# Input norm and MLP norm of a decoder layer: transposes one tile ahead, a split gain row, and row factors moved behind the MLP

## The chip, the cores and the metric

The kernel runs on one core of a Trainium2 chip. A run's time is the device time of one execution in microseconds. The profile is one execution taken by the hardware profiler; its span runs from the first to the last instruction.

## The reference, cut to what matters

One decoder layer on 512 tokens of width 1024, in float32. An RMS norm feeds one wide projection, whose parts go to an mLSTM branch and to a sliding-window attention branch. The two are gated, merged and projected back onto `x`. Then a squared-ReLU MLP, a gated per-layer input and a last RMS norm follow.

```
def rmsnorm(x, g):
    return x * rsqrt(mean(x * x, axis=-1) + EPS) * g

h = rmsnorm(x, norm_mix_g);  proj = h @ w_in          # 1024 -> 6664, split into nine parts
...                                                    # mLSTM branch y_a, window attention y_b
merged = sigmoid(g_a) * (y_a @ w_branch_a) + sigmoid(g_b) * (y_b @ w_branch_b)
x = x + merged @ w_out
u = rmsnorm(x, norm_mlp_g) @ w_up                      # 1024 -> 4096
x = x + square(relu(u)) @ w_down                       # 4096 -> 1024
gate = sigmoid(rmsnorm(x, norm_ple_g) @ w_ple_gate)
x = x + gate * (p @ w_ple_proj)
return rmsnorm(x, final_norm_g)
```

## The kernel before, in words

Each big product is made of three products of fp32r parts. `split` casts a value to its high part on ScalarE (L134) and subtracts to get the low part on VectorE (L135); `pairs` then gives high x high, high x low and low x high. Weights arrive on SyncE's DMA queue as raw tiles `wr`, four at a time, and become `wh` and `wl`. The program is written as plain calls; a scheduler that works with estimated durations sets the order of each engine's queue when the kernel is built. `tc.issue_after(ins)` adds an edge of order, without a wait: what the block issues on that instruction's engine comes behind it. `tc.keep_in_program_order` pins an instruction's place.

**The input norm (L249 to L292).** The four tiles of 128 tokens come in as `xt`. The gain row `grow` is spread over all partitions by two plain float32 products with a row of ones (L251), into the PSUM tile `gmix`. For each tile, ScalarE squares and sums (L268), takes the root (L256), VectorE takes the reciprocal (L258) and makes `xn = x * rs * gmix` in two halves (L272). TensorE transposes `xn` in eight blocks into two PSUM banks (L279). Each bank is split into the high and low part of `h`, and ScalarE copies it once more into `hf`, the full-precision `h` (L284). Then come the 24 products of the tile with the weight `w_vsif`, which was split in three pieces by `load_w` within tile 0, and the results `vs` and `gt` are taken out. `hf` is read later by the sums `s1` to `s4`, which the value and gate projections use.

**The MLP (L841 to L977).** `x1` holds the transposed, gain-scaled `x` in parts, without the row factor of the norm. The row factors `rstd` of the four tiles are spread to all partitions by four plain products with a scaled identity `dg` (L859) into `rB`. The MLP goes in four quarters, each an up stage and a down stage. In `up`, 24 products fill a PSUM bank, VectorE makes `max(ps, 0) * rB` (L879), ScalarE squares it into `F` (L883), and sums of blocks of `F` are split into `uf`. `down` uses seven products per block instead of eight, with the PSUM pairs X, Y and Z. Each finished pair is added to `x` in one 1024-wide add (`acc`, L916); the product `p1` that several blocks share is summed over the quarters and added three times in the last one (`acc_p1`).

Of the kernel before, what the change touches and what calls it, by code (L numbers as in the profile page):

```python
# [16 lines left out]
P = 128  # L17
# [19 lines left out]
def block_kernel(  # L37
# [59 lines left out]
    def ps_a():  # L97
        return pp.tile([P, 1024], F32, tag="a", bufs=2, name=nm("psa"))
# [29 lines left out]
    def r32(t):  # L128
        return t.bitcast(F32)
# [66 lines left out]
    V.memset(ones, 1.0)  # L196
    eps_t = cp.tile([P, 1], F32, name="eps_t")

    cp.tile([P, 24], F32, name="pad")
    V.memset(eps_t, EPS)  # L200
    zeros4 = c1.tile([4, P], F32, name="zeros4")
    V.memset(zeros4, 0.0)
# [43 lines left out]
    nc.sync.dma_start(out=bif, in_=b_if.broadcast_to([P, 8]))  # L246
    sink = c1.tile([P, 16], F32, name="sink")
    nc.sync.dma_start(out=sink, in_=sinks.broadcast_to([P, 16]))
    gmix = ps_a()  # L249
    for c in range(2):  # L250
        T.matmul(gmix[:, c * 512 : (c + 1) * 512], ones[:1, :], grow[:, c * 512 : (c + 1) * 512], start=True, stop=True)  # L251
    def rstd_of(ss, n):

        w = ss.shape[1]
# [6 lines left out]
    vs = []  # L261
    gt = c1.tile([P, NT, 8], F32, name="gt")
    h2, hT = big_hl("h")
    hf = []
    for m in range(NT):
        xn = tok_scratch("xn")
        ss = small("ss", 1)
        A.activation(xn, xt[m], AF.Square, accum_out=ss)  # L268
        rs = rstd_of(ss, D)
        for c in range(2):  # L270
            o = slice(c * 512, (c + 1) * 512)
            V.scalar_tensor_tensor(xn[:, o], xt[m][:, o], rs, gmix[:, o], ALU.mult, ALU.mult)  # L272
        hf.append(tk("hf")[:, :D].rearrange("p (k c) -> p k c", k=KT))
        if m == 0:
            wv = [load_w(None, (k.stop - k.start) * 264, k.stop - k.start, w) for k, w in zip(K3, wv)]
        for kq in range(2):
            ps = ps_t()
            for k in range(4):
                T.transpose(ps[:, k * P : (k + 1) * P], xn[:, kq * 512 + k * P : kq * 512 + (k + 1) * P], ident)  # L279
            split(  # L280
                [t[:, 4 * kq : 4 * kq + 4, m * P : (m + 1) * P] for t in h2],
                ps.rearrange("p (k c) -> p k c", k=4),
            )
            A.copy(hf[m][:, 4 * kq : 4 * kq + 4, :], ps.rearrange("p (k c) -> p k c", k=4))  # L284

        ps = ps_g()
        for c in range(3):
            mm_tok(ps[:, :264], wv[c], hT[K3[c]], m, first=c == 0, last=c == 2)
        t = sp.tile([P, 256], F32, tag="vs", bufs=4, name=nm("vs"))
        A.copy(t, ps[:, :256])  # L290
        V.tensor_add(gt[:, m, :], ps[:, 256:264], bif)
        vs.append(t)  # L292

    def proj_T(wd, i, bank=ps_g):
# [77 lines left out]
    o_proj(1)  # L372


    vm = []
    for m in range(NT):
        t = tk("vm").rearrange("p (h d) -> p h d", h=NH)
        G.memset(t[:, :, DV : DV + 1], 1.0)
        vm.append(t)

    def h_part(tok, par):

# [52 lines left out]
    def seven(form, prod, X, Y, Z, b, post):  # L435


        b11, b12, b21, b22 = b
        n = range(len(b11))
        for i in n:  # L440
            prod(X, A11, form(b11[i]), i, True)
        post("p1", X)
        for i in n:
            V.tensor_sub(b12[i], b22[i], b12[i])
            V.tensor_add(b11[i], b12[i], b11[i])
        for i in n:
# [18 lines left out]
        post("c21", Y)  # L465

    def vml():
        raws = quads(w_vml, ["wr", "wr", "lm", "lm", "wr", "wr", "lm", "lm"])
# [380 lines left out]
    rB = mp.tile([P, 512], F32, name="rB")  # L849
    p1 = np_.tile([P, 2, 512], F32, name="p1")  # L850

    psr = pair()[:, 0, :]
    for m in range(NT):
        junk = np_.tile([P, 7 * 256], F32, tag="uf", bufs=8, name=nm("junk"))[:, :D]
        ss = small("ss", 1)
        A.activation(junk, xk[m], AF.Square, accum_out=ss)
        dg = mp.tile([P, 512], F32, tag="rt", bufs=3, name=nm("dg"))[:, :P]
        V.tensor_scalar_mul(dg, ident, rstd_of(ss, D))
        T.matmul(psr[:, m * P : (m + 1) * P], ones, dg, start=True, stop=True)  # L859
    A.copy(rB, psr)  # L860

    def load_down(q):
        raws = []
# [9 lines left out]
    def up(q, uf):  # L873
        fs = None
        for f in range(8):
            ps = ps_g()
            mm_T(ps, load_w(w_up[q * 8 + f], KT * P, KT), x1)
            a = mp.tile([P, 512], F32, tag="rt", bufs=3, name=nm("rt"))
            V.scalar_tensor_tensor(a, ps, 0.0, rB, ALU.max, ALU.mult)  # L879
            if f % 2 == 0:  # L880
                fs = F()
            o = 2 * (f % 2)
# [14 lines left out]
    def down(q, uf):  # L897
# [13 lines left out]
                    ops += pairs([h[:, o : o + P] for h in uf[2 * kh + k]], [h[:, k, :] for h in w])  # L911
                chain(ps[:, t, :], ops, first and kh == 0, last and kh == 1, True)

        def acc(ps, toks, n):
            o = XK[:, 2 * toks : 2 * toks + 2, n * 512 : (n + 1) * 512]
            return V.tensor_add(o, ps, o)  # L916

        def acc_p1(toks, n):
            if q == 3:
                tc.keep_in_program_order(acc(p1, toks, n))  # L920

        for kh in range(2):
            V.tensor_sub(b12[kh], b22[kh], b12[kh])
# [261 lines left out]
```

## Time and profile before

| what | value |
|---|---|
| median of three runs | 908.59 us (907.73, 908.59, and one of 1108.4) |
| the profiled execution, its own time | 907.79 us |
| its span | 906.0 us |
| TensorE busy | 890.4 us, 98% of the span |
| weight loads on TensorE | 739.4 us |
| VectorE busy | 640.6 us, 71% |
| ScalarE busy | 452.8 us, 50% |
| GpSimd busy | 25.0 us, 3% |
| DMA | 101.51 MB, mean 112 GB/s |

The busy time of an engine is the time in which one of its instructions runs. Engines work side by side, so these times overlap. A row of a group gives the line, the engine, the operation, what it writes and reads with shapes, the count, then the busy time and the mean of one in nanoseconds, and then the idle time ahead of it with what ended that. A row of the chain gives a start, a length, and the engine and line that set the end there. A row of the timeline gives a start, a length and the instruction, and in brackets the idle time ahead of it. Names are as in this page: PE is TensorE, PEld its weight loads, DVE VectorE, ACT ScalarE, POOL GpSimd, SP SyncE.

### The profile page before, as it was taken

What the parts mean: (1) busy time and instruction counts of PE and PEld (TensorE: products, weight loads), DVE (VectorE), ACT (ScalarE), POOL (GpSimd) and SP (SyncE); (2) the same over time, 40 slices, a digit from 0 to 9 for tenths busy, and PEclk for the clock granted to TensorE, in tenths of its full rate; (3) what the DMA queues carried; (4) which work ended last, traced back from release to release, by engine and by line L of the source; (5) the groups of instructions that cost most, each with busy time, mean ns of one, the idle gap of its engine ahead of it and who ended that gap; (6) DMA issues with size and microseconds to landing.
All of it is one profiled execution on the core that took longest, in us unless ns stands there. A gap on an engine that the chain in (4) does not pass through costs nothing.

```text
span 906.0 us, 11754 instructions
## 1 busy us (share of the span) xinstructions
PE 890.4 (98%) x4490; PEld 739.4 (82%) x4490; DVE 640.6 (71%) x1020; ACT 452.8 (50%) x757; POOL 25.0 (3%) x44
## 2 busy tenths in 40 slices
PE   7999999999999999999999999999999999999996
PEld 5888889998877677777888888888888888888886
DVE  6684687874787977466654678857966895799556
ACT  6573444454677567564322545334434533454753
POOL 0011000000000000000210000000000000000000
PEclk9999999999999999999999999999999999999998
DMA  6644124435211122234452520531162044201402
GB/s 235 241 156 151 59 81 167 162 117 173 71 49 69 47 96 92 76 110 140 163 186 93 207 95 1 198 127 47 54 225 94 0 159 146 69 24 64 145 1 93
DMA packets 30346, 101.51 MB, mean 112 GB/s; under 512 B 4301, under 2 KB 4813, under 8 KB 30290
## 3 DMA queue, kind: packets, MB, share of 16 engines
q1 hardware_dynamic: 28002, 93.15, 29.9%
q0 software_dynamic: 2144, 7.35, 2.3%
q8 instruction: 35, 0.57, 0.2%
q10 hardware_dynamic: 144, 0.26, 0.1%
q14 instruction: 21, 0.17, 0.1%
HBM read 91.30 MB, written 8.40 MB: 110 GB/s over the span
## 4 chain that ended last, share of the span: by engine, by line
PE 93%; ACT 2%; DVE 2%; DMA 1%; issue 0%; SPq 0%; ACTq 0%; DVEq 0%
PE psg L162 51%; PE psp L162 23%; PE psa L162 10%; PE pst L724 2%; PE pst L653 1%; PE pst L162 1%; PE psa L645 1%; PE pst L714 1%; PE psa L608 1%; PE psa L609 1%; DMA xt<-in_x 1%; DMA gfin<-in_g_fin 1%; PE psp L817 1%; ACT jk L736 1%; ACT pT L647 0%
## 5 line engine op out<-in xcount | busy, mean ns | idle before, releaser
L134 ACT CAST wh<-wr 128x1024 fp32r<-128x1024 f32 (+1 forms) x137 | 142.9, 1046 | 207.7 <-PE psg L162 75.4
L135 DVE TENSOR_TENSOR wl<-wr,wh 128x1024 fp32r<-128x1024 f32 (+1 forms) x137 | 173.4, 1270 | 102.4 <-ACT wh L134 95.4
L162 PE MATMUL psg<-x,wh 128*128 128x512 f32 x512 | 158.4, 390 | 0.0
L162 PE MATMUL psp<-wh,uf 128*128 128x512 f32 x448 | 139.2, 390 | 0.0
L162 PEld LDWEIGHTS psg<-x,wh 128*128 128x128 f32 x512 | 96.1, 188 | 19.8
L162 PE MATMUL psg<-h,wh 128*128 128x512 f32 x320 | 101.3, 395 | 0.0
L162 PE MATMUL psg<-x,wl 128*128 128x512 f32 x256 | 99.7, 390 | 0.0
L162 PEld LDWEIGHTS psp<-wh,uf 128*128 128x128 f32 x448 | 84.1, 188 | 17.4
L162 PE MATMUL psp<-wl,uf 128*128 128x512 f32 x224 | 87.3, 390 | 0.0
L134 ACT CAST wh<-wd 128x1024 fp32r<-128x1024 f32 x44 | 46.3, 1054 | 58.0 <-PE psp L162 26.1
L162 PEld LDWEIGHTS psg<-h,wh 128*128 128x128 f32 x320 | 58.8, 188 | 15.9 <-issue 4.9
L162 PE MATMUL psg<-h,wl 128*128 128x512 f32 x160 | 62.9, 393 | 0.0
L135 DVE TENSOR_TENSOR wl<-wd,wh 128x1024 fp32r<-128x1024 f32 x44 | 53.5, 1219 | 4.4 <-ACT wh L134 4.1
L162 PEld LDWEIGHTS psg<-x,wl 128*128 128x128 f32 x256 | 48.1, 188 | 9.8
L162 PE MATMUL psa<-h,wh 128*128 128x256 f32 (+1 forms) x256 | 55.2, 312 | 0.0
L162 PEld LDWEIGHTS psp<-wl,uf 128*128 128x128 f32 x224 | 42.1, 188 | 8.6
L135 DVE TENSOR_TENSOR uf<-F,uf 128x1792 fp32r<-128x1792 f32 (+2 forms) x20 | 33.0, 1650 | 21.8 <-ACT uf L134 21.8
L162 PEld LDWEIGHTS psa<-h,wh 128*128 128x128 f32 x256 | 41.9, 191 | 3.5 <-ACT p L533 0.7
L162 PE MATMUL psg<-yb,wh 128*128 128x512 f32 x128 | 42.8, 409 | 0.0
L134 ACT CAST uf<-F 128x1792 fp32r<-128x1792 f32 (+2 forms) x20 | 27.9, 1395 | 26.4 <-DVE F L893 26.2
L162 PE MATMUL psg<-ya,wh 128*128 128x512 f32 x128 | 40.6, 394 | 0.0
L879 DVE SCALAR_TENSOR_TENSOR rt<-psg,rB 128x512 f32<-128x512 f32 x32 | 22.0, 688 | 25.6 <-PE psg L162 25.6
(273 smaller groups left out, 1673.3 us busy)
## 6 DMA issues: line engine op xcount, KB each, us to landing
wr<-in_w_up SPq DMA_DIRECT2D x32, 512.0 KB, 3.2
wd<-in_w_down SPq DMA_DIRECT2D x24, 512.0 KB, 3.8
wr<-in_w_o SPq DMA_DIRECT2D x8, 512.0 KB, 4.5
gd<-gr POOLq DMA_DIRECT2D x8, 512.0 KB, 2.9
wr<-in_w_qsw SPq DMA_DIRECT2D x8, 512.0 KB, 4.3
wr<-in_w_qkml SPq DMA_DIRECT2D x8, 512.0 KB, 3.3
wr<-in_w_b SPq DMA_DIRECT2D x8, 512.0 KB, 3.2
gl<-gd SPq DMA_DIRECT2D x8, 512.0 KB, 3.4
```

The costliest lines, as they stand in the source:

```text
L134: A.copy(dst[0], src)
L135: V.tensor_sub(dst[1], src, r32(dst[0]))
L162: last_mm[0] = T.matmul(ps, l, r, start=first and i == 0, stop=last and i == len(ops) - 1, skip_group_check=parts)
L608: T.matmul(o, q[:, n * P : (n + 1) * P], kk[kp][ab][:, k0 : k0 + 256], start=True, stop=False)
L609: T.matmul(o, q[:, n * P : (n + 1) * P], kl[kp][ab][:, k0 : k0 + 256], start=False, stop=True)
L645: T.transpose(pt[:, c : c + P], lm3[ab][:, g, j * P : (j + 1) * P], ident)
L653: T.matmul(o[HALF[ab], :], vs[n + 1 - nk + j][:, c : c + 64], pTs[j][:, ab * 512 : (ab + 1) * 512], start=j == 0, stop=j == nk - 1,)
L714: T.matmul(psc[:, n0:], qk[4 + h][:, n0 : n0 + P], qk[h][:, n0:], start=True, stop=True)
L724: T.matmul(pn[:, : DV + 1], wT[s][:, t * P : (t + 1) * P], vm[s][:, h, :], start=s == 0, stop=s == t)
L736: A.activation(jk[:, :DV], h_of(h, t), AF.Square, scale=rd[:, t : t + 1], accum_out=hss[:, h, t : t + 1])
L817: T.transpose(ps[:, m * P : (m + 1) * P], xk[m][:, k * P : (k + 1) * P], ident)
L879: V.scalar_tensor_tensor(a, ps, 0.0, rB, ALU.max, ALU.mult)
```

## The change

In the input norm:

- `grow` is split into two fp32r parts, and `gmix` is the sum of four fp32r products with an fp32r row of ones, in place of two plain ones. Nine plain 128x128 products of ones with ones (`stir`) stand before, between and behind them.
- The loop over tiles is taken apart into `norm` and `columns`. The norm and the transposes of tile m+1 are written ahead of the products of tile m. Odd tiles transpose into one two-bank tile and are cast, subtracted and copied 1024 wide.
- The high part of `w_vsif` is made by GpSimd. The low part of its first piece is ordered behind tile 0's norm on VectorE, the other two behind tile 1's norm. Tile 1's norm is ordered behind tile 0's casts on ScalarE, tile 2's behind tile 1's subtraction on VectorE.
- `hf` of tiles 1 to 3 is copied by ScalarE as before; `hf` of tile 0 is the sum of both parts of `h`, made by VectorE after the last `gt`. `vm` takes its buffers later.

In the MLP: the factors `r2 = 1 / (mean(x*x) + EPS)` stay one column per tile. The rectifier runs on ScalarE without a factor, and since relu(u r)^2 = r^2 relu(u)^2, the factor is applied to the rows of the down products, as each accumulation into `x` becomes two 512-wide `ps * r2 + x`. `rB`, `dg` and the four products go.

```diff
+    idle = ps_g()
+
+    def stir(n):
+        for i in range(n):
+            tc.keep_in_program_order(T.matmul(idle[:, :P], ones, ones, start=True, stop=True))
+
+    one_row = c1.tile([1, P], F32R, name="one_row")
+    A.copy(one_row, ones[:1, :])
     gmix = ps_a()
+    gparts = [[act_r("gm")[:1, :] for _ in range(2)] for _ in range(2)]
     for c in range(2):
-        T.matmul(gmix[:, c * 512 : (c + 1) * 512], ones[:1, :], grow[:, c * 512 : (c + 1) * 512], start=True, stop=True)
+        split(gparts[c], grow[:, c * 512 : (c + 1) * 512])
+    stir(5)
+    for i in range(2):
+        for c in range(2):
+            tc.keep_in_program_order(
+                T.matmul(gmix[:, c * 512 : (c + 1) * 512], one_row, gparts[c][i], start=i == 0, stop=i == 1, skip_group_check=True)
+            )
+        stir(1 if i == 0 else 3)
...
+    def norm(m):
         xn = tok_scratch("xn")
         ss = small("ss", 1)
         A.activation(xn, xt[m], AF.Square, accum_out=ss)
         rs = rstd_of(ss, D)
         for c in range(2):
             o = slice(c * 512, (c + 1) * 512)
-            V.scalar_tensor_tensor(xn[:, o], xt[m][:, o], rs, gmix[:, o], ALU.mult, ALU.mult)
+            done = V.scalar_tensor_tensor(xn[:, o], xt[m][:, o], rs, gmix[:, o], ALU.mult, ALU.mult)
+        return xn, done.ins
...
+    def columns(m, xn):
+
+        if m % 2:
+            ps = ps_a()
+            halves = [ps[:, :512], ps[:, 512:]]
+        else:
+            halves = [ps_t(), ps_t()]
+        for k in range(KT):
+            T.transpose(halves[k // 4][:, k % 4 * P : (k % 4 + 1) * P], xn[:, k * P : (k + 1) * P], ident)
+        n = 8 if m % 2 else 4
+        for k in range(0, KT, n):
+            dst = [t[:, k : k + n, m * P : (m + 1) * P] for t in h2]
+            src = (ps if m % 2 else halves[k // 4]).rearrange("p (k c) -> p k c", k=n)
+            first = A.copy(dst[0], src)
+            second = V.tensor_sub(dst[1], src, r32(dst[0]))
+            if m:
+                if k == 0:
+                    hf.append(tk("hf")[:, :D].rearrange("p (k c) -> p k c", k=KT))
+                A.copy(hf[m][:, k : k + n, :], src)
+        return first.ins, second.ins
+
+    def load_vs_w(c):
+        n = K3[c].stop - K3[c].start
+        hl = [wp.tile([P, 1024], F32R, tag=t, bufs=WB, name=nm(t))[:, : n * 264] for t in ("wh", "wl")]
+        G.tensor_copy(hl[0], wv[c][:, : n * 264])
+        V.tensor_sub(hl[1], wv[c][:, : n * 264], r32(hl[0]))
+        return [q.rearrange("p (k c) -> p k c", k=n) for q in hl]
+
+    xn, normed = norm(0)
+    with tc.issue_after(normed):
+        wv[0] = load_vs_w(0)
+    on_scalar, _ = columns(0, xn)
+    with tc.issue_after(on_scalar):
+        xn, normed = norm(1)
+    with tc.issue_after(normed):
+        wv[1:] = [load_vs_w(1), load_vs_w(2)]
+    _, on_vector = columns(1, xn)
+    for m in range(NT):
+        if m == 1:
+            with tc.issue_after(on_vector):
+                xn, _ = norm(2)
+            columns(2, xn)
+        elif m == 2:
+            columns(3, norm(3)[0])
         ps = ps_g()
         for c in range(3):
             mm_tok(ps[:, :264], wv[c], hT[K3[c]], m, first=c == 0, last=c == 2)
...
+    hf[0] = tk("hf")[:, :D].rearrange("p (k c) -> p k c", k=KT)
+    with tc.issue_after(gate_in.ins):
+        hi, lo = [r32(t[:, :, :P]) for t in h2]
+        V.tensor_add(hf[0], hi, lo)
...
-        dg = mp.tile([P, 512], F32, tag="rt", bufs=3, name=nm("dg"))[:, :P]
-        V.tensor_scalar_mul(dg, ident, rstd_of(ss, D))
-        T.matmul(psr[:, m * P : (m + 1) * P], ones, dg, start=True, stop=True)
-    A.copy(rB, psr)
+        V.tensor_scalar(ss, ss, 1.0 / D, EPS, ALU.mult, ALU.add)
+        V.reciprocal(r2[:, m : m + 1], ss)
...
-            V.scalar_tensor_tensor(a, ps, 0.0, rB, ALU.max, ALU.mult)
+            A.activation(a, ps, AF.Relu)
...
-        def acc(ps, toks, n):
-            o = XK[:, 2 * toks : 2 * toks + 2, n * 512 : (n + 1) * 512]
-            return V.tensor_add(o, ps, o)
+        def acc(ps, toks, n, pin=lambda i: None):
+            for t in range(2):
+                o = xk[2 * toks + t][:, n * 512 : (n + 1) * 512]
+                pin(V.scalar_tensor_tensor(o, ps[:, t, :], r2[:, 2 * toks + t : 2 * toks + t + 1], o, ALU.mult, ALU.add))
```

More of the change, by code (lines that the diff above doesn't have):

```diff
@@ L197, in block_kernel @@
     eps_t = cp.tile([P, 1], F32, name="eps_t")
-    cp.tile([P, 24], F32, name="pad")
+    cp.tile([P, 16], F32, name="pad")
     V.memset(eps_t, EPS)
@@ L263, in block_kernel @@
     h2, hT = big_hl("h")
-    hf = []
-    for m in range(NT):
+    hf = [None]
+    def norm(m):
         xn = tok_scratch("xn")
@@ L271, in block_kernel @@
             o = slice(c * 512, (c + 1) * 512)
[L272 to L284, printed above, removed]
+            done = V.scalar_tensor_tensor(xn[:, o], xt[m][:, o], rs, gmix[:, o], ALU.mult, ALU.mult)
@@ L290, in block_kernel @@
         A.copy(t, ps[:, :256])
-        V.tensor_add(gt[:, m, :], ps[:, 256:264], bif)
+        gate_in = V.tensor_add(gt[:, m, :], ps[:, 256:264], bif)
         vs.append(t)
@@ L372, in block_kernel @@
     o_proj(1)
[L375 to L379, printed above, removed]
+    hf[0] = tk("hf")[:, :D].rearrange("p (k c) -> p k c", k=KT)
+    with tc.issue_after(gate_in.ins):
+        hi, lo = [r32(t[:, :, :P]) for t in h2]
+        V.tensor_add(hf[0], hi, lo)
     def h_part(tok, par):
@@ L465, in seven @@
         post("c21", Y)
+    vm = []
+    for m in range(NT):
+        t = tk("vm").rearrange("p (h d) -> p h d", h=NH)
+        G.memset(t[:, :, DV : DV + 1], 1.0)
+        vm.append(t)
     def vml():
@@ L848, in block_kernel @@
     A21, A11, A22, A12, S1, S2, S3, S4 = range(8)
-    rB = mp.tile([P, 512], F32, name="rB")
     p1 = np_.tile([P, 2, 512], F32, name="p1")
-    psr = pair()[:, 0, :]
+    r2 = cp.tile([P, NT], F32, name="r2")
     for m in range(NT):
```

2 lines of the change are left out of this document (1 added, 1 removed).

## The prediction

> **What bounds the kernel now.** I read the page first (busy times, then the chain that ended last), then the chain by pieces in time, then the timeline of the two places that the diff touches, then the groups by line, and last the busy time by stretch.
>
> ```profile
> span 906.0 us, 11754 instructions
> PE 890.4 (98%) x4490; PEld 739.4 (82%) x4490; DVE 640.6 (71%) x1020; ACT 452.8 (50%) x757; POOL 25.0 (3%) x44
> PE 93%; ACT 2%; DVE 2%; DMA 1%; issue 0%; SPq 0%; ACTq 0%; DVEq 0%
> ```
>
> TensorE is busy for 890.4 of 906.0 us and carries 93% of the chain. So only two things can move the end: work taken off TensorE, and the 15.6 us in which it stands idle or runs slowly. VectorE and ScalarE are off the path wherever TensorE is full. The largest hole is at the start. The chain by pieces shows it:
>
> ```profile
> 2.50 6.10 DMA xt<-in_x
> 8.62 1.15 ACT xn L268 x2
> 9.77 0.48 ACT h L134
> 10.29 5.93 PE psg L162 x24
> 16.22 0.79 PE pst L279 x4
> 17.04 0.59 ACT h L134
> 17.65 0.70 DVE h L135
> 18.40 2.94 PE psg L162 x22
> ...
> 27.96 2.93 PE psg L162 x22
> ```
>
> Three things are to be seen. First, the cast of the first `h` (9.77) is queued on ScalarE behind the square of the second x tile, which waits for its transfer until 8.62. Second, the 24 products of tile 0 take 5.93 us, those of later tiles 22 in 2.94: 0.25 against 0.13 us each, so TensorE runs at half rate until about 16 us. Third, tiles 1 and 3 begin 9.56 us apart, so each takes 4.78, of which the products are 2.94; the other 1.8 are transposes and the cast and subtraction behind them (0.79, 0.59, 0.70 ahead of tile 1), in series.
>
> **The change part by part.** The sum is made against the profiled execution, 907.79 us by its own time, 906.0 its span; the 1.8 us around the span stay. The median of the three runs shown is 908.59, so 0.8 above it.
>
> *Input norm.* Tile 0 first.
>
> ```profile
> 6.33 1.41 DVE L272 SCALAR_TENSOR_TENSOR xn<-xt,rs,psa 128x512 f32<-128x512 f32 x2
> 7.22 1.94 PE L279 MATMUL pst<-ident,xn 128*128 128x128 f32 x8 [1.19 <-DVE xn L272]
> L284 ACT COPY hf<-pst 128x512 f32<-128x512 f32 x8 | 4.7, 587 | 0.6 <-DVE h L135 0.6
> L256 ACT ACTIVATE sd<-ss,eps_t 128x1 f32<-128x1 f32 x12 | 3.3, 296 | 0.1
> L135 DVE TENSOR_TENSOR wl<-wr,wh 128x792 fp32r<-128x792 f32 x2 | 2.0, 984 | 0.5 <-ACT wh L134 0.4
> L647 ACT COPY pT<-psa 128x1024 f32<-128x1024 f32 x14 | 14.1, 1013 | 5.2 <-PE psa L645 5.2
> L916 DVE TENSOR_TENSOR xk<-psp,xk 128x1024 f32<-128x1024 f32 x24 | 29.3, 1221 | 5.7 <-PE psp L162 5.7
> 21.17 1.04 PE L279 MATMUL pst<-ident,xn 128*128 128x128 f32 x8
> ```
>
> The norm of tile 0 still ends at 7.74, and its transposes at half rate give their first bank at about 8.3 and the second at 9.2. The square of tile 1 is now ordered behind both casts, and the weights' casts leave ScalarE for GpSimd. So the casts (0.587 each, taken from the copy of the same bank) run at 8.3 and 9.2 and end at 9.8, instead of starting at 9.77. Then tile 1: square and its read-out 1.15, to 10.95; square root 0.30, to 11.25; the reciprocal and the hand-overs about 0.35; norm 1.41: about 13.0. VectorE then makes the low parts of weights 2 and 3, 0.98 and, with two thirds of the columns, about 0.7, to 14.7. Tile 0's last six products wait for them and end at 15.4 (at 0.13 each) or 16.2 (at 0.25). Meanwhile tile 1 is transposed by 13.5, cast in one 1024-wide copy (1.01, from the nearest row of that width) by 14.6, and subtracted (1.22) by 15.9. Its products start there instead of at 18.40. From then on the next tile's transposes stand between the products, and the casts lie beside them, so three tiles cost 3 x 3.1 for products (24 at 0.13) and 2 x 0.95 for transposes: 11.2, to 27.1. Before, the last products ended at 27.96 + 2.93 = 30.9. **Gain 3.8 us.** ScalarE has per tile 1.15 + 0.30 + 1.01 + 1.01 and the copy of `vs`, some 3.9 us, about as much as TensorE's 4.05: the cover is thin but there.
>
> What else is issued there. The gain row's two plain products become four over split halves, with stirring products before, between and behind. ScalarE copies them while it would wait for x.
>
> ```profile
> 2.29 3.75 PE L251 MATMUL psa<-grow,ones 1*128 1x512 f32 x4 [2.29 <-DMA grow<-in_g_mix]
> L791 POOL TENSOR_TENSOR sga<-sga,gb 128x512 f32<-128x512 f32 x8 | 11.2, 1401 | 242.9 <-ACT wh L134 228.2 <-DVE sga L790 10.6 <-issue 4.1
> L206 POOL TENSOR_SCALAR_AFFINE_SELECT band<-band 128x256 f32<-128x256 f32 x1 | 0.4, 394 | 0.0
> ```
>
> Each of these four passes took 0.94 for 512 columns. I count a product of split halves as half a pass (the lower end; a whole one is the upper), and a stir as two passes of a quarter of the width: 4 x 0.47 and 9 x 0.47, 6.1 us in all, from about 1 us, where `ones` is filled, to 7.2. `gmix` is done three stirs earlier, at 5.8, ahead of the 6.33 where it is read; at the upper end it comes 1.3 late. A one-input GpSimd copy of 792 columns isn't in the trace. Scaled by columns from the fill of 256 it takes 1.2 us, from the two-input add of 512 it takes 2.2; I take 1.5, nearer the fill, which also reads one tensor. The first weight's high part is then there at about 8.8, before its low part and `h` are wanted; at 2.2 it pushes the first `h` subtractions and the norm behind them by 0.3 to 0.4. `hf` of tile 0 becomes one VectorE add (about 1.2), and its two ScalarE copies go; VectorE has that much free before the sums over `hf` are wanted by the value projection, 40 us later.
>
> The Trainium skill, "GPSIMD Engine Reference", section Engine selection, says that one-input work runs there at about line rate; an estimate from that page's 1.2 GHz is 0.7 us for 792 columns, and the sum would stay as it is.
>
> *MLP norm.* The four products that spread the row factors go, with four scalings, the square roots and the copy `rB`. What they cost TensorE stands in the chain around them:
>
> ```profile
> 514.58 0.44 PE psp L859 x4
> 515.02 0.92 PE psg L162 x4
> 515.95 0.37 PE psp L859 x2
> 516.32 0.24 PE psg L162
> 516.56 0.23 PE psp L859 x2
> 516.78 3.43 PE psg L162 x15
> ```
>
> 0.44 + 0.37 + 0.23: **gain 1.04 us**, all of it on the path. In exchange the up stage's rectifier moves from VectorE to ScalarE, and each accumulation into `x` becomes two scaled ones.
>
> ```profile
> L879 DVE SCALAR_TENSOR_TENSOR rt<-psg,rB 128x512 f32<-128x512 f32 x32 | 22.0, 688 | 25.6 <-PE psg L162 25.6
> L860 ACT COPY rB<-psp 128x512 f32<-128x512 f32 x1 | 0.6, 574 | 0.0
> L883 ACT ACTIVATE F<-rt 128x512 f32<-128x512 f32 x32 | 20.1, 628 | 20.7 <-DVE rt L879 20.7
> L138 DVE SCALAR_TENSOR_TENSOR x<-psp,gmlp,x 128x512 fp32r<-128x512 f32 x8 | 5.6, 747 | 2.4 <-ACT x L137 2.3
> 554.70:592.80 38.10, 38.10 (x169) 31.54 (x168) 31.84 (x31) 17.89 (x19) 0.00 (x0) 1.00 0.40 138
> 592.80:636.30 43.50, 43.50 (x193) 36.05 (x192) 29.58 (x35) 17.76 (x19) 0.00 (x0) 1.00 0.21 73
> 799.50:839.00 39.50, 39.48 (x180) 32.38 (x179) 36.79 (x42) 18.70 (x26) 0.00 (x0) 1.00 0.18 56
> ```
>
> (In the stretches the columns are TensorE, weight loads, VectorE, ScalarE, GpSimd.) In an up stage of 43.5 us ScalarE has 17.8; eight rectifiers at 0.57 (the PSUM copy) to 0.63 (the square) add 4.8, so TensorE covers them. In a down stage two scaled adds at 0.747 take 1.49 where one took 1.22: 0.27 more, six times a quarter, nine times in the last. VectorE goes from 31.8 to 33.5 of 38.1, and in the last quarter from 36.8 to some 38.5 of 39.5 (0.27 x 9, less one rectifier of 0.69). That is the tight place, priced at nothing because of these two rows:
>
> ```profile
> 831.97 1.22 DVE L135 TENSOR_TENSOR wl<-wr,wh 128x1024 fp32r<-128x1024 f32 x1
> 838.40 0.39 PE L162 MATMUL psp<-wh,uf 128*128 128x512 f32 x1
> ```
>
> The last low part that a down product needs is there at 833.2, and the products that read it are the last twelve, at 0.227 each from 835.9: 2.7 us of slack against seven earlier adds of 0.27 = 1.9.
>
> The sum: 907.79 - 3.8 - 1.0 = **903.0 us**.
>
> **The rivals.** *The order keeps the tiles in series.* The transposes of the next tile are written ahead, but if they come to stand behind the products on TensorE's queue, the period of 4.78 stays. Tile 0 would still end 0.8 earlier, and 1.04 come from the MLP: 907.79 - 1.8 = 906.0. For it: the order is computed from estimated durations, and TensorE takes its queue in order. Against it: the low parts of weights 2 and 3 come after tile 1's norm on VectorE, so tile 1's transposes are ready before tile 0's products can end.
>
> *The clock rises before tile 0.* The stirs fill TensorE from about 1.2 us on; if full rate is reached by 7.2, the eight transposes take 1.04 instead of 1.94 and everything behind them comes up to 0.9, say 0.7, earlier: 902.3. Against it: in the trace of before, 3.75 us of products at 2.29 did not bring it; 5.9 us of products from 10.29 did. The Trainium skill, "TensorE: Matmul & The Clock Gate", Part 1, says that about 3.4 us of sustained work release a gate that is at half rate by default, and Part 4 there says that transposes don't count as such work; the 5.9 us agree with a free-running window of that length, the 3.75 of one-row products don't, unless one-row products don't count either.
>
> *The wider adds pace the down stages (the slower side).* If VectorE's lag reached TensorE in full, the price would be 27 adds by 0.27 = 7.3 us, at the low parts of each quarter's fourth to sixth product: 903.0 + 7.3 = 910.3, slower than before. It decides from the point where the lag at the last low part of a quarter exceeds its 2.7 us of slack. The last quarter's 38.5 of 39.5 speaks for it; the 4 to 5 us that VectorE has free in the other three, and that no wait of TensorE is on the chain there now, speak against.
>
> **How the numbers follow.** The forecast has 0.60, the series 0.20, the early clock 0.10, the paced down stages 0.07, and 0.03 for what I don't see. One unknown remains for all cases, since the whole order is computed anew: what TensorE waits for elsewhere. The longest such wait after the start is
>
> ```profile
> PE psa L645 <- ACT pT L647: 1.6, 1, 1.6
> ```
>
> and with the others of 0.2 that makes about 2 us that a new order may save or add. The range: downwards, the early clock less these 2.0: 900.3. Upwards, the series with 0.4 for a slow GpSimd copy, 0.3 for `gmix` (between its ends 0 and 1.3, nearer the lower) and these 2.0: 908.7. What lies beyond is most of the paced down stages, under 0.1. A change of 2% is 18 us (about what a measurement of this kernel can tell from no change). All cases lie well inside it: TensorE's whole idle time is 15.6 us, and no cost above reaches 18. So 0.02 faster, 0.96 within, 0.02 slower.
>
> **What would show it.** Right: the weight projection after the norm starts near 27 instead of 30.9; tile 1's products start near 16; no casts of `h` behind a wait for x; no L859 products, and the up stage's products run on without a break; VectorE in the last quarter near 38.5 with TensorE still full. Wrong: a tile period near 4.8 us, a hole in TensorE inside a down stage ended by a low part or an accumulation, table loads at the rectifier, or a TensorE start at half rate beyond 16 us.

## The result, and the profile after

The changed kernel takes 905.88 us in the median of 16 runs (904.81 to 907.32), the kernel before 907.26 in as many. The ratio, made from fast runs alone, is 0.9981, with a 95% interval of 0.9974 to 0.9987. By it the time fell by about 1.7 us (1.4 between the medians) where 4.8 were forecast. The profiled execution fell from 907.79 to 905.84 us, its span from 906.0 to 904.1.

The page of the changed kernel, its span and busy times:

```profile
span 904.1 us, 11781 instructions
PE 890.4 (98%) x4500; PEld 741.6 (82%) x4500; DVE 627.0 (69%) x1016; ACT 466.9 (52%) x778; POOL 28.1 (3%) x47
```

TensorE's busy time didn't move, although products went: the idle matmuls fill time that was empty. So the page can't say where the time went. For that the two traces were laid side by side, product by product on TensorE. The difference of the start times, after less before, is a running account:

| place in the kernel | forecast for this place | start before, after | account after it |
|---|---|---|---|
| input norm, first product of the projection behind it | -3.8 | 30.72, 28.03 | -2.7 |
| gates of the branches | 0 | 421.61, 418.47 | -3.1 |
| first product of `w_out` | 0 | 462.35, 460.37 | **-2.0** |
| first up stage, just ahead of the norm's products | 0 | 514.18, 512.36 | -1.8 |
| first up stage, behind the norm | -1.04 | 516.86, 513.96 | **-2.9** |
| the four quarters of the MLP | 0 | | within 0.5 of that |
| last transposes of `x` for the per-layer gate | 0 | 847.33, 845.59 | **-1.7** |

The two parts of the change gave 2.7 and 1.1. Two places that the diff doesn't touch took back 1.1 and 1.2. The 0.4 gained at the gates was not pursued.

**The input norm.** The timeline of TensorE in the changed kernel, and of VectorE and GpSimd at the rows that matter:

```profile
6.51 1.65 PE L254 MATMUL psg<-ones 128*128 128x128 f32 x6
7.95 1.92 PE L302 MATMUL pst<-ident,xn 128*128 128x128 f32 x8
9.78 0.56 PE L162 MATMUL psg<-wh,h 128*128 128x264 f32 x1
11.30 0.59 PE L162 MATMUL psg<-wl,h 128*128 128x264 f32 x1 [0.96 <-DVE wl L319]
...
13.45 1.91 PE L302 MATMUL psa<-ident,xn 128*128 128x128 f32 x8
...
17.72 0.51 PE L162 MATMUL psg<-wh,h 128*128 128x264 f32 x2 [0.24 <-DVE h L308]
...
28.03 0.63 PE L162 MATMUL pst<-h,wh 128*128 128x512 f32 x2
```

```profile
6.91 1.41 DVE L291 SCALAR_TENSOR_TENSOR xn<-xt,rs,psa 128x512 f32<-128x512 f32 x2
9.67 0.69 DVE L308 TENSOR_TENSOR h<-pst,h 128x512 fp32r<-128x512 f32 x1 [1.35 <-ACT h L307]
10.27 0.97 DVE L319 TENSOR_TENSOR wl<-wr,wh 128x792 fp32r<-128x792 f32 x1
7.22 0.84 POOL L318 CAST wh<-wr 128x792 fp32r<-128x792 f32 x1 [4.59 <-DMA wr<-in_w_vsif]
```

The overlap is as forecast: tile 1 is transposed before tile 0's last products, and no cast waits for x any more. The sizes differ. Tile 0's norm starts at 6.91 (6.33 before). TensorE waits 0.96 for the first weight's low part, which stands behind the first `h` subtraction on VectorE, although GpSimd's high part was done at 8.06. The eight transposes of tile 1 still take 1.91, which is half rate, and end at 15.36; the forecast had tile 1 transposed by 13.5. So tile 1's products run on from 17.72, where 15.9 was forecast. The three tiles from there on took 10.3 us, 0.9 less than forecast.

**The MLP.** The chain at the norm, then the busy times in a down stage, an up stage and the last down stage (TensorE, weight loads, VectorE, ScalarE, GpSimd):

```profile
509.99 0.44 PE psp L877 x4
510.43 9.58 PE psg L162 x42
551.80:589.80 38.00, 38.00 (x169) 31.48 (x168) 32.15 (x34) 18.37 (x19) 0.00 (x0) 1.00 0.42 139
589.80:633.30 43.50, 43.50 (x194) 36.02 (x193) 25.31 (x29) 21.56 (x26) 0.00 (x0) 1.00 0.22 73
796.40:836.50 40.10, 40.00 (x181) 32.63 (x180) 37.33 (x48) 19.23 (x26) 0.00 (x0) 1.00 0.14 43
```

The products run on without the breaks for L859, and TensorE is full in all three stretches. VectorE is busy for 37.3 of 40.1 us in the last one, where some 38.5 of 39.5 were forecast.

**The two losses.** At 460 us, TensorE (two rows) and VectorE of the changed kernel, then TensorE and VectorE of the kernel before at the same place:

```profile
459.10 0.39 PE L162 MATMUL psg<-ya,wl 128*128 128x512 f32 x1
460.37 0.47 PE L162 MATMUL psp<-wh,mg 128*128 128x512 f32 x1 [0.88 <-ACT wh L134]
459.53 0.69 DVE L850 TENSOR_TENSOR sga<-psg,gl 128x512 f32<-128x512 f32 x1 [1.65 <-PE psg L162]
...
462.35 0.39 PE L162 MATMUL psp<-wh,mg 128*128 128x512 f32 x1
462.55 0.69 DVE L790 TENSOR_TENSOR sga<-psg,gl 128x512 f32<-128x512 f32 x1 [1.65 <-PE psg L162]
```

In the changed kernel the first product into a new accumulator waits 0.88 us; before, it started ahead of VectorE's read. The row names ScalarE's weight cast as the releaser. But VectorE's read of the last `psg` ends at 460.22, just ahead of it. In the allocation of the changed kernel `psg` has PSUM banks 0 and 1, and the first `psp` takes banks 0 and 1. Before, `psg` had 6 and 7. PSUM is the memory that the products here are written to, in eight banks from 0 to 7. The allocation gives the lowest banks to the kind of tile that is asked for first: before, that was the two-bank kind of `gmix`, in the changed kernel it is the new `idle = ps_g()`.

At 842 us, VectorE, SyncE's queue and TensorE of the changed kernel, then the same engines of the kernel before:

```profile
839.23 1.23 DVE L135 TENSOR_TENSOR wl<-wr,wh 128x1024 fp32r<-128x1024 f32 x1
842.92 0.69 DVE L1047 TENSOR_SCALAR glast<-gfin 128x1024 f32<-128x1024 f32 x1 [2.46 <-DMA gfin<-in_g_fin]
843.52 0.75 DVE L138 SCALAR_TENSOR_TENSOR x<-psp,gple,x 128x512 fp32r<-128x512 f32 x1
836.60 0.33 SPq L1044 DMA_DIRECT2D gfin<-in_g_fin  x1
844.33 0.66 PE L877 MATMUL psp<-ident,xk 128*128 128x128 f32 x4 [0.54 <-DVE x L138]
845.59 0.66 PE L877 MATMUL psp<-ident,xk 128*128 128x128 f32 x4 [0.60 <-DVE x L138]
...
844.66 0.69 DVE L988 TENSOR_SCALAR glast<-gfin 128x1024 f32<-128x1024 f32 x1 [2.16 <-DMA gfin<-in_g_fin]
838.82 0.33 SPq L985 DMA_DIRECT2D gfin<-in_g_fin  x1
847.33 0.66 PE L817 MATMUL psp<-ident,xk 128*128 128x128 f32 x4 [0.20 <-DVE x L138]
```

VectorE stops for the final scale's transfer, with the subtractions that free the PSUM pairs behind it, and the transposes wait for those. The kernel before stopped there too (2.16 us), but TensorE then waited only 0.2. In the changed kernel the scale is there 1.7 us earlier than before (842.92 for 844.66), while TensorE comes to these transposes 2.9 earlier. Its transfer goes out behind three of the nine transfers of `w_pg`; before, behind four.

### The profile page after: what moved, and what is told of

It reads as the page before. It is cut to its first block, busy times and chain, and to the rows that moved or that the text cites. A ratio compares the mean times of both kernels' runs of the same rounds, so it can differ in the third digit from the quotient of the medians.

```text
span 904.1 us, 11781 instructions
## 1 busy us (share of the span) xinstructions
PE 890.4 (98%) x4500; PEld 741.6 (82%) x4500; DVE 627.0 (69%) x1016; ACT 466.9 (52%) x778; POOL 28.1 (3%) x47
## 4 chain that ended last, share of the span: by engine, by line
PE 73%; ACT 2%; DVE 2%; DMA 1%; issue 0%; SPq 0%; ACTq 0%
PE psg L162 42%; PE psp L162 22%; PE pst L784 2%; PE pst L713 1%; PE psa L705 1%; PE pst L774 1%; PE psa L162 1%; PE psa L668 1%; PE psa L669 1%; DMA gfin<-in_g_fin 1%; PE psp L877 1%; ACT jk L796 1%; ACT wh L134 1%; ACT pT L707 0%; DMA ptok<-in_p 0%
## 5 line engine op out<-in xcount | busy, mean ns | idle before, releaser
L135 DVE TENSOR_TENSOR wl<-wr,wh 128x1024 fp32r<-128x1024 f32 x134 | 170.7, 1279 | 131.0 <-ACT wh L134 124.4
L134 ACT CAST wh<-wr 128x1024 fp32r<-128x1024 f32 x134 | 140.9, 1053 | 208.5 <-PE psg L162 85.6
L162 PEld LDWEIGHTS psg<-h,wh 128*128 128x128 f32 x320 | 58.7, 188 | 15.9 <-issue 4.9
L162 PE MATMUL psa<-h,wl 128*128 128x256 f32 (+1 forms) x128 | 39.6, 309 | 0.0
```

Source lines behind the costliest of these rows:

```text
L134: A.copy(dst[0], src)
L135: V.tensor_sub(dst[1], src, r32(dst[0]))
L162: last_mm[0] = T.matmul(ps, l, r, start=first and i == 0, stop=last and i == len(ops) - 1, skip_group_check=parts)
```

## The experiments

Ratios are to the kernel before, run beside each on the same chip (its medians were 906.7 to 907.4), with 95% intervals. So ratios are compared below, rather than medians. In the text each kernel has the name of its run: `e1` to `e9` and `e13` to `e16`, as marked in the table.

| kernel | median, us | ratio |
|---|---|---|
| the changed kernel | 905.88 | 0.9981 [0.9974, 0.9987] |
| input norm's part alone (e1) | 905.35 | 0.9982 [0.9974, 0.9991] |
| MLP norm's part alone (e2) | 907.50 | 1.0006 [0.9997, 1.0014] |
| changed, banks as before (e3) | 903.92 | 0.9968 [0.9956, 0.9981] |
| changed, final scale's products later (e4) | 904.44 | 0.9964 [0.9950, 0.9977] |
| changed, both repairs (e5) | 902.72 | 0.9954 [0.9942, 0.9966] |
| both, low part first (e6) | 902.18 | 0.9950 [0.9938, 0.9962] |
| both, no idle matmuls (e7) | 902.73 | 0.9954 [0.9942, 0.9966] |
| both, single adds, row factors left out (e8) | 902.67 | 0.9954 [0.9943, 0.9966] |
| both, low part first, no idle matmuls (e9) | 903.41 | 0.9955 [0.9939, 0.9970] |
| both, gain row on 128 rows (e13) | 903.34 | 0.9951 [0.9937, 0.9965] |
| the same as e13, low part first (e14) | 902.48 | 0.9946 [0.9932, 0.9961] |
| the same as e14, ten idle matmuls behind (e16) | 902.36 | 0.9953 [0.9940, 0.9967] |
| changed, gain row on 128 rows (e15) | 905.25 | 0.9979 [0.9969, 0.9988] |

**The two halves of the change, each alone** (the diff cut between the input norm and the MLP).

> Only the input norm's part of the change, in the kernel before; the norm on the MLP's sums is left as it was. Before is 907.3 us, after 905.9. Theory A (the two traces): the weight projection starts 2.6 to 2.7 us earlier than before, at about 28.0 in place of 30.7, and 1.1 us of that is lost near 460 us, where the first product of the last projection into a fresh accumulator waits for VectorE's read of the last gate bank, which this part's first allocation has put into the same PSUM bank. The tail is as before. Sum: -1.5 to -2.0, 905.3 to 905.8 us. Rival B: the loss near 460 us belongs to the later part or to chance; then -2.6, 904.7 us, and that first product waits only for ScalarE.

> Only the norm on the MLP's sums; the input norm as before. Theory A: the MLP's norm gives 0.85 to 1.05 us at about 516 us, the quarters lose nothing, and the tail, where the final scale's transfer now goes out ahead of one weight load and VectorE stops for it with four subtractions behind, loses 1.0 to 1.3 us: sum -0.1 to +0.4 us, 907.2 to 907.7. No loss near 460 us. Rival B: the tail's loss in the changed kernel comes from the earlier clock of its input norm, not from this part; then -0.9 to -1.0, 906.3 us. Rival C: the additions of 0.74 us in place of 0.6 do slow the quarters in kernels that reach them later; then above 908.

Theory A held for both. The input norm alone gives what the whole change gives, and the MLP's part alone gives nothing. In their traces the first has the wait at 460 us (0.9) and no wait in the tail, the second has none at 460 and 0.9 in the tail. The final scale's transfer stands behind four transfers of `w_pg` in the first, as before, and behind three in the second. The MLP's products gave about 1.1 in the second too (its account goes from -0.5 ahead of the norm's products to -1.6 behind them).

The start of the weight projection moves from execution to execution, and with it the account: it is 27.22 in the first, where 28.0 was expected, and 30.04 in the second, whose input norm is that of the kernel before (30.72).

**Banks as before.**

```diff
-    idle = ps_g()
+    idle = ps_a()
```

> The changed kernel with one allocation altered: the bank that the idle matmuls write is taken from the two-bank accumulators, so that the banks of all later tiles are those of the kernel before; every engine's order of instructions is the same as in the changed kernel. Theory A (bank): the first product near 460 us no longer waits for VectorE; 1.0 to 1.1 us come back, 904.8 us where the changed kernel has 905.9. Rival B (the page names ScalarE's copy of that product's weight as its releaser): the weight's copy is what is late, the product waits for it in either bank, and the time stays at 905.9 within 0.3.

The ratio puts this kernel 1.2 us below the changed one, as theory A has it; its median, 903.92, comes out lower than that. The same place in this kernel's trace:

```profile
458.10 0.39 PE L162 MATMUL psg<-ya,wl 128*128 128x512 f32 x1
458.33 0.39 PE L162 MATMUL psp<-wh,mg 128*128 128x512 f32 x1
458.53 0.69 DVE L850 TENSOR_TENSOR sga<-psg,gl 128x512 f32<-128x512 f32 x1 [1.65 <-PE psg L162]
```

The product now starts before VectorE's read has begun, while ScalarE's cast of the weight runs beside it (458.30 to 459.36). So the bank was the cause and not the weight that the row named. The tail is reached 2.6 us earlier in this profile than in the changed kernel's (1.0 by the bank, 0.85 by an earlier start), and there TensorE's wait for the subtractions rose from 1.1 to 1.8 us: the next wait in line took part of the gain.

**The final scale's products later.** The two `tensor_scalar_mul` that write `glast` and `gfin` move behind the last `columns_of`:

```diff
+    with tc.issue_after(low.ins):
+        V.tensor_scalar_mul(glast, gfin, D**0.5 / 8192)
+        V.tensor_scalar_mul(gfin, gfin, -(D**0.5) / 8192)
```

> The changed kernel with VectorE's two multiplications of the final scale moved behind the last of the eight subtractions of the transposed residual; the transfer itself is issued as before. Theory A: VectorE's stop of 2.46 us at 840.5 goes, the transposes there wait under 0.3 us in place of 1.1, and 0.9 to 1.3 us come back: 904.6 to 905.0 us where the changed kernel has 905.9. Rival B: the end is set by the weight loads that follow the scale's transfer in the queue (five of them over 19.4 us), so that what is won here is waited for again at the gate's products: 905.9 within 0.3.

Theory A held, with a little more than it has (1.5 us by the ratios); TensorE waits for nothing there now. VectorE's timeline shows that the subtraction that was stuck until 843.52 starts three us earlier:

```profile
840.41 1.40 DVE L138 SCALAR_TENSOR_TENSOR x<-psp,gple,x 128x512 fp32r<-128x512 f32 x2
848.53 0.68 DVE L1062 TENSOR_SCALAR glast<-gfin 128x1024 f32<-128x1024 f32 x1
```

**Both repairs, and on top of them three single edits.**

> The changed kernel with both repairs: the idle matmuls' bank taken from the two-bank accumulators, and the final scale's two multiplications behind the last subtraction. Alone the first gave 903.9 and the second 904.4 us where before had 906.9 (and the changed kernel, by its ratio, 905.2). Theory A: they lie at different places (460 and 842 us) and add: -1.1 to -1.3 and -0.9 to -1.1 from 905.2, so 902.8 to 903.2 at a before of 906.9, a ratio near 0.996 or lower (0.9955). Rival B: the ends meet the same bound (the weight loads of the gate); then no better than the better one alone, 903.9.

The repairs add (902.72). The interval of each repair alone still overlaps that of the changed kernel; with both it doesn't. The edit of the next is one pair of instructions that change places on VectorE.

> The kernel with both repairs, and the low part of the first weight put ahead of the first `h` subtraction on VectorE (one pair of instructions changes places, nothing else). Theory A: TensorE's wait of 1.0 us at 10.3 us (tile 0's second product, for that low part) goes; but the transposes of tile 1 wait for that tile's norm on VectorE, which ends at 13.0 to 13.5, so most is given back: a gain of 0 to 0.5 us over the kernel with both repairs. Rival B: the hole at 10.3 is also what keeps the clock low; without it the full rate comes at 11.7 or earlier in every run (it came at 11.65 and 11.70 in two profiles and at 15.5 and 15.7 in two others of the same start), and the gain is 0.8 to 1.3 us.

0.5 us in the medians, as theory A allows, but the two intervals overlap. In its profile the rate rose at 11.7. It rose as early in two profiles with the hole (e1 and e3, at 10.4 and 10.3 us), so an early rise doesn't need the hole's removal, and the gain is below rival B's 0.8.

> The kernel with both repairs, without the nine idle matmuls (the gain row's four products stay); the order on every other engine is the same. Theory A: the idle matmuls are what lets the full rate come at 11.7 us in a part of the executions, so without them it comes at 15 us or later always: tile 1's transposes run at half rate (1.9 us), and the median is 0.3 to 0.8 us higher than with them. Rival B: the moment of the full rate is a matter of a window that the products alone fill, and falls at 11.7 or 15.6 by chance, with or without the idle matmuls: no difference beyond 0.2 us.

No difference (902.73). TensorE's queue shows what the idle matmuls cost. Without them tile 0's transposes start when the norm gives them their first half; with them (6.50 to 8.15) they stand behind these:

```profile
7.32 1.94 PE L294 MATMUL pst<-ident,xn 128*128 128x128 f32 x8 [2.22 <-DVE xn L283]
```

That is 0.63 us earlier than 7.95, given up for a clock that came early in only three of the seven profiles that start with idle matmuls and one-row products. The traces' records of the granted clock have its first rise at 10.3, 10.4 and 11.7 in those (e3, e1, e6), and between 14.5 and 15.6 in the other four (the changed kernel, e4, e5, e8). With the early rise the weight projection starts at 27.2 in all three, with the late one at 27.8 to 28.3. Without idle matmuls the rise came at 14.1 here and at 16.5 in e9. Whether the idle matmuls bring the early rise at all isn't shown by so few profiles.

> The kernel with both repairs, with the accumulations of the down stages made in one addition of 1024 columns again, as before the change; this leaves out the row factors. It frees 0.27 us of VectorE for each of 27 accumulations, 7.3 us in all. Theory A: VectorE is off the path there, so the quarters take as long: 0 within 0.4 us; the order near the end also goes back to that of before (the final scale's transfer one place later, the residual's transposes ahead of the last projection), which the repaired kernel no longer feels. Rival B (wider adds pace the down stages): TensorE's small holes in the down stages close, and 1 us or more is won, up to 7.3.

No difference (902.67): the wider accumulations cost nothing, as priced. This kernel leaves out the row factors, so it doesn't compute the layer and serves for its time alone. The final scale's transfer went back behind four transfers of `w_pg`, as before the change, so its place in the order follows from the estimated lengths of the adds.

> Both repairs, the first weight's low part ahead of the first `h` subtraction, and no idle matmuls. So far, at a before of 907.1 us: both repairs 902.7, with the low part ahead 902.2, with both repairs and no idle matmuls 902.7 (its tile 0 transposed 0.63 us earlier, at 7.32). Theory A: the idle matmuls cost 0.6 us of start and give about as much by the clock, and the low part's place gives 0.5 in either version: 902.0 to 902.3, no better than with the idle matmuls. Rival B: the low part's gain came from the clock alone (full rate at 11.8 in that profile), which the idle matmuls brought; then without them no gain, 902.7. Rival C: the 0.6 us and the 0.5 add: 901.6 or less.

A ratio of 0.9955: no gain. Rival C isn't seen; between the other two it decides nothing. The transfer of x was late in its profile (tile 0's square at 5.37; 4.51 to 5.4 over all profiles, whatever the kernel).

**The clock alone.** These three were run once each, for their traces (910.99, 919.61 and 905.25 us).

> The kernel with both repairs, with 40 idle matmuls (fp32, 128 rows, 128 columns, two passes each) in place of the first five: a measurement of the clock alone, everything behind comes later. Theory A: full-width products count as work, so the rate of the passes doubles 3.4 to 7 us after the first at 1.05, between 4.5 and 8; the 40 take about 13 us. Rival B: idle matmuls of 128 columns don't count; they stay at 0.25 us a pass and take 20 us.

> The same with 40 one-row products (fp32, 1 row, 128 columns) in place of the first five idle matmuls. Theory A: one-row products don't count as work (3.75 us of them brought no full rate in the kernel before): they stay at half rate for all 20 us, and the full rate comes only with the products behind them. Rival B: they count like others, the rate doubles between 4.5 and 8, and the 40 take about 13 us.

> The same with 40 transposes of the 128x128 identity in place of the first five idle matmuls. Theory A: transposes don't count as work (the Trainium skill, "TensorE: Matmul & The Clock Gate", Part 4, says so; no run here has shown it yet): half rate for all 20 us. Rival B: they count, and the rate doubles between 4.5 and 8 (the first transposes start at about 1.6, when the identity is there).

The three rows of the 40 instructions:

```profile
1.05 12.03 PE L254 MATMUL psa<-ones 128*128 128x128 f32 x80 [1.05 <-DVE eps_t L200]
1.05 17.43 PE L263 MATMUL psa<-ones 1*128 1x128 f32 x80 [1.05 <-DVE eps_t L200]
1.57 6.05 PE L263 MATMUL psa<-ident 128*128 128x128 f32 x40 [1.57 <-POOL ident masks.py:199]
```

Single passes went from 0.213 to 0.112 us 5.9 us after the first idle matmul, and to 0.109 us 3.1 us after the first transpose. The one-row products stayed at 0.213 to the end. So theory A held for the first two, and rival B for the transposes: idle matmuls and transposes both count as work for the clock, one-row products don't, and those of the gain row interrupt the work that the clock sees. The Trainium skill, "TensorE: Matmul & The Clock Gate", Part 4, says that transposes don't; here the measurement decides against it, for transposes of this kernel's kind.

**The gain row over 128 rows** (the halves of `g` in zero-filled tiles).

> The kernel with both repairs, with the gain row's four products made over 128 rows in place of one (the halves of `g` lie in tiles that are zero but for their first row, so the result is the same); the order on TensorE is unchanged, VectorE fills four tiles with zeros first. It replaces the only passes ahead of tile 0's products that count as no work for the clock (one-row products: 17 us of them brought no full rate; full-width products did after 5.9 us, transposes after 3.1). Theory A: the full rate comes by 8 us in every run; tile 0's transposes take about 1.0 us in place of 1.9, tile 1's 1.0, and the weight projection starts near 26.5 in place of 27.2 to 28.0: 0.8 to 1.5 us less than with both repairs alone, a ratio of 0.994 or lower where those had 0.9954. Rival B: the start is paced by ScalarE and VectorE (square, casts, norm) and not by TensorE's rate: transposes at full rate, but less than 0.4 us gained. Rival C: the zero fills delay the gain row by a microsecond or more, and what the clock gives is lost.

> The same with the first weight's low part ahead of the first `h` subtraction. Theory A: with TensorE at full rate from tile 0 on, the wait for that low part (1.0 us at 10.3) is on the path, and its removal adds 0.3 to 0.6 us: ratio near 0.9935. Rival B: tile 1's norm ends at 13.0 to 13.5 in either case and paces the tile: no difference beyond 0.2 us.

> The changed kernel as it is, with the gain row's products over 128 rows, and neither repair: the input norm's part of the prediction with the clock alone mended. Theory A: its start comes to the gain forecast for it, 3.8 us or more against before (weight projection at 26.9 or earlier where before has 30.7), and the time falls from 905.2 or so by 0.8 to 1.5 us. Rival B: the missing 1.1 us are not the clock's (the x transfer 0.6 later, the low part's place): projection still at 27.5 or later, under 0.4 us.

> Both repairs, the gain row over 128 rows, the low part ahead, and ten idle matmuls behind the gain row in place of three. In the three profiles with the gain row over 128 rows the full rate came by 5.5 us, but TensorE then stood idle for 1.4 to 2.2 us until tile 0's norm, and in two of the three the rate was half again for tile 0 or its products. Seven more idle matmuls (14 passes of 0.112 us at full rate) fill 1.6 us of that. Theory A: the rate holds through tile 0 and tile 1, the projection starts at 26.6 to 26.9, and the median is 0.3 to 0.8 us below that with three (ratio 0.9946): 0.994 or lower. Rival B: at most 0.2 us, since the norm's chain on ScalarE and VectorE, and the transfer of x, pace the start by then. Rival C: where the rate is still half, the seven cost 3 us and hold tile 0's transposes back, to 10 us: slower.

All four brought the full rate early, at 4.1 and 4.4 us in e14 and e15 and at 6.1 and 6.7 in e13 and e16 (the text on e16 has 5.5 for the first three; e13's 6.1 is later). In two of them it was lost again where TensorE stood idle. From e13, which kept the rate behind the first idle time of 1.44 and lost it by the end of the second; below the rows, three stretches with the granted clock in the third column from the end:

```profile
8.06 1.22 PE L305 MATMUL pst<-ident,xn 128*128 128x128 f32 x8 [1.44 <-DVE xn L294]
11.38 0.59 PE L162 MATMUL psg<-wl,h 128*128 128x264 f32 x1 [1.44 <-DVE wl L322]
13.52 1.91 PE L305 MATMUL psa<-ident,xn 128*128 128x128 f32 x8
...
6.20:9.50 3.30, 1.69 (x13) 1.15 (x12) 1.73 (x4) 1.41 (x5) 0.84 (x1) 1.00 1.01 373
9.60:16.30 6.70, 5.26 (x23) 4.96 (x24) 5.31 (x8) 4.96 (x10) 2.17 (x2) 0.50 0.93 288
16.40:20.00 3.60, 3.54 (x28) 3.20 (x28) 3.18 (x7) 2.63 (x6) 0.00 (x0) 1.00 0.84 314
```

In e15 it was gone by tile 0, after 2.0 us idle. With the low part ahead (e14) it held through an idle time of 2.2, and with that time filled as well (e16) tile 0 and tile 1 ran at full rate too:

```profile
8.32 1.04 PE L305 MATMUL pst<-ident,xn 128*128 128x128 f32 x8
12.53 1.22 PE L305 MATMUL psa<-ident,xn 128*128 128x128 f32 x8 [0.97 <-DVE xn L294]
26.74 0.62 PE L162 MATMUL pst<-h,wh 128*128 128x512 f32 x2
```

There the projection starts 4.0 us earlier than before, 26.93 in e14, 27.80 and 28.36 in e15 and e13. So theory A failed for e13 and e15, whose rate didn't hold. For e14 and e16 the trace came out as theory A has it and the time didn't: their intervals, and that of e13, overlap that of the kernel with both repairs, and e15's that of the changed kernel. A gain by the clock of up to 1 us is seen in the traces alone. Of all kernels run, those with both repairs are the fastest, and which of them is the best can't be told.

## Why the prediction was wrong, step by step

- **The order elsewhere, priced at nothing within 2.0 us either way: the step that failed.** It cost 2.3 us, and both costs follow from the diff. The prediction had no term for the allocation of `idle`, but its place ahead of `gmix` changed the bank of every later tile of the first part; `psg` came to lie under the first new accumulator, which cost 1.1. And the longer accumulations changed the order that the scheduler makes near the end, so that the final scale's transfer no longer comes early enough for TensorE: 1.2. Both waits are shown, by e3, e4 and both together in e5. That the second comes from the accumulations is seen in e1 and e2: with the old ones TensorE comes 2.6 us earlier than before and waits for nothing, with the new ones it comes 1.5 earlier and waits 0.9.
- **The input norm, 3.8: mechanism right, size off by 1.1 in the profiled execution.** 0.2 of that is the start before, 30.72 and not 30.9. The term that was mis-sized is the one for tile 1's transposes. They were taken as done by 13.5 us, at full rate, although the prediction itself has half rate until about 16 us; they ended at 15.36, at half rate. In the three profiles with an early clock (e1, e3, e6) the projection starts at 27.2, which is the forecast's 27.1; with a late one the forecast isn't reached. Two other things were later than forecast and cost little. The low part's place behind `h` gives a wait of 1.1 in e1 and e3 and none in e6, and their projections start within 0.05 us of each other. And x landed later (tile 0's square started at 5.14, before at 4.55), but tile 0's transposes stand behind three idle matmuls and start near 7.95 in all seven profiles with this start; this place in the queue made the second bank come at 9.87 and not 9.2, and tile 1's norm end at 13.51 and not 13.0. Where the rate held from tile 0 on, the trace gave 3.8 (e14) and 4.0 (e16). All of these gains are against the one start at 30.72; with the same input norm e2 has 30.04. GpSimd's copy, taken as 1.5 us with bounds of 1.2 and 2.2, took 0.84: below both bounds, and near the estimate of 0.7 by the Trainium skill, "GPSIMD Engine Reference", section Engine selection. Its earlier end brought nothing, as the low part was queued elsewhere.
- **The MLP norm, 1.04: right** (1.1 in the account, from -1.8 to -2.9).
- **The wider accumulations, nothing: right.** VectorE was busy for 37.3 of 40.1 us in the last quarter; taking the width away changed nothing (e8).
- **The rivals.** The tiles didn't stay in series. The early clock came in a part of the executions, at 10.3 to 11.7 where the rival had 7.2, and it was needed to reach the forecast's start at all. Nothing paced the down stages. The time, 905.9, lies inside the stated range and near the rival of the tiles in series, but for another reason; the change was about a third of the forecast one.
- With both repairs the kernel takes 902.7, close to the 903.0 of the sum. That is not a proof of the sum: the second repair also removes a stop that the kernel before had, and the trace gains 0.5 at the gates, which was neither forecast nor explained.

## What to carry to other kernels

A new tile can move every later one to another bank, so for each first write into a new accumulator, look which engine read that bank last; the row's named releaser may be only the one that came next to it. When a small change in durations is all that a stage gets, look at the places where the scheduler puts an instruction that waits for a transfer ahead of those that TensorE needs. A gain on TensorE is worth its full size only until the next wait in line: here the tail took back 0.7 us in the profile of the first repair until it was repaired too.

## What the hardware showed that was not expected

- One-row products (1x128, fp32) don't raise TensorE's rate in 17 us; full-width ones do after 5.9, transposes after 3.1. The Trainium skill, "TensorE: Matmul & The Clock Gate", Part 1, describes a free-running window of about 3.4 us, by which the moment varies between executions; that it varied here from 10.3 to 15.6 us for one start agrees in kind, but is more than one such window.
- The granted clock changes in steps of 3.41 us. In its records, the stretch at full clock behind the first rise and the stretch at half clock behind that last 3.41 and 6.83 us in e13 and in e15, 13.65 and 3.41 in e10, 10.24 and 3.41 in e12: one, two, three or four times 3.41.
- In e13 and e15 the granted clock fell to 0.50 at the end of a stretch of 3.41 us in which TensorE was busy for 1.69 and 1.34 of 3.3 us, with idle times of 1.4 and 2.0; in e14 it survived an idle time of 2.2. The Trainium skill, "TensorE: Matmul & The Clock Gate", Part 1, has the fall come after at least one idle window of about 3.4 us; here less idle time was enough, and the measurement decides. What made e14 differ no run here shows.
- Ahead of its first record the granted clock of a stretch reads 1.00, at half rate too: in the changed kernel from 8.00 to 15.60, where a product of 264 columns takes 0.22 us and not 0.12. There the rate has to be read from the length of the passes.
